# A hybrid attention backbone on one core: the opening of layer 0 rewritten, from the first load to the values

## The chip, the cores and the metric

The kernel runs on one NeuronCore of a Trainium2 chip. The metric is device time in microseconds, from one execution of the program. The engines are TensorE (PE in the profile, with its weight loads as PEld), VectorE (DVE), ScalarE (ACT), GpSimd (POOL) and SyncE (SP), which issues most of the DMAs. Each engine takes its own instructions in order and waits for others by semaphores.

## The reference

The model has two layers over 1024 latent tokens and 256 context tokens of width 1024. The opening that this case is about computes, for layer 0, the adaptive norm of both streams and then the projection to queries, keys, values and gates. Values are the first columns to be projected.

```python
shift_x, scale_x, gate_x = adaln(c, ada_w[i], ada_b[i])
shift_c, scale_c, gate_c = adaln(c_ctx, ada_w[i], ada_b[i])
hx = rms_norm(x, norm_g[i]) * (1.0 + scale_x[:, None]) + shift_x[:, None]
hc = rms_norm(ctx, norm_g[i]) * (1.0 + scale_c) + shift_c
...
q, k, v, g = jnp.split(h @ w_in, [A_WIDTH, A_WIDTH + A_KV_WIDTH, A_WIDTH + 2 * A_KV_WIDTH], axis=-1)
```

Here `adaln` is `silu(cond) @ w + bias` split into three parts of 1024 columns. Layer 0 goes on with windowed attention with a sink, layer 1 with latent attention, and a last RMS norm ends the model. All inputs are float32. Products that need full precision are split into a high and a low part (`hi` is the value rounded to the type float32r, `lo` the rest), and three products of the parts (`mm3`: L126, L127, L128) take the place of one.

## The kernel before

Tokens are in ten tiles of 128 (two of context, then eight latent), and tiles are handled in five pairs `p`. For each tile, `norm_x` (L174 to L182) loads 128 x 1024 values, squares and sums them on ACT (L178), makes the factor `(mean + eps) ** -0.5` in two small POOL operations (L179, L180), and multiplies the tile by it on DVE (L181). `turn_x` transposes the tile on TensorE in eight pieces of 128 x 128 (L188) and copies them from PSUM with ACT (L189), so that channels lie on partitions. `build_h` then applies scale and shift for each 128 channels, on DVE in place (L202), rounds two channel blocks to `hi` on ACT (L205), and subtracts to get `lo` on DVE or POOL (L207).

Scale and shift come from `ada_mm`: the weight matrix is 1024 x 2048 here, loaded in halves `h` of 512 columns for scale and for shift. The stationary operand is the two conditioning columns, so a product fills two rows of PSUM (rows 0 and 32, L337). `ada_cols` copies the rows from PSUM on ACT (L341), transposes them (L344) and adds the bias and the norm's weight. The first half's columns are ready before the second half's weights have all been loaded. `half0` builds four channel blocks of h for pairs 0 and 1, and multiplies them into the values' sums, which stay open in PSUM until the second half is done. Pairs 2 to 4 run through `build_x`, `build_h` and `proj_a`.

The weights of the projection are cut into ten blocks of 256 columns. Block 0 holds the values (1280 to 1536) and is multiplied with tokens on the output's partitions; its sums are split into hi and lo in `V` (L121, L122). Block 1 (query columns) and those behind it are turned the other way (`proj_t`): the first piece of a block covers the context in products of 256 columns, the next two pieces cover the latent tokens in products of 512. `fetch` loads a block's weights in four pieces and `cut` splits them on ACT and POOL, driven by `next_item`, which counts the pieces of work. `ada_vec` computes what is left of both layers' conditioning on DVE (L383, L385), one or two steps a piece.

Up to the end of block 0 a scheduler orders each engine's instructions. From the loop over `order` on, `tc.manual_schedule()` keeps the order in which the code is written.

Of the kernel before, what the change touches and what calls it, by code (L numbers as in the profile page):

```python
# [18 lines left out]
D = 1024  # L19
# [4 lines left out]
NP = TOK // 256  # L24
EPS = 1e-6
# [34 lines left out]
def kernel(ctx: ExitStack, tc: tile.TileContext, t, out, dbg=None):  # L60
# [58 lines left out]
    def split(hi, lo, src, lo_eng=None):  # L119

        nc.scalar.copy(hi, src)  # L121
        (lo_eng or nc.vector).tensor_sub(lo, src, hi.bitcast(F32))  # L122

    def mm3(o, a, b, first, last):
        (ah, al), (bh, bl) = a, b
        nc.tensor.matmul(o, ah, bh, start=first, stop=False)  # L126
        nc.tensor.matmul(o, al, bh, start=False, stop=False)  # L127
        nc.tensor.matmul(o, ah, bl, start=False, stop=last)  # L128
# [69 lines left out]
    def build_h(p, xt, hT, A, B, fast=False, ks=range(8)):  # L198

        w = 1 if p == 0 else 0  # L200
        for k in ks:
            nc.vector.tensor_scalar(xt[:, k, :], xt[:, k, :], A[:, k, w : w + 1], B[:, k, w : w + 1], ALU.mult, ALU.add)  # L202
            if k % 2:
                hi = hT[:, 0, k - 1 : k + 1, :]
                nc.scalar.copy(hi, xt[:, k - 1 : k + 1, :])  # L205
                eng = nc.vector if fast or k % 4 == 1 else nc.gpsimd
                eng.tensor_sub(hT[:, 1, k - 1 : k + 1, :], xt[:, k - 1 : k + 1, :], hi.bitcast(F32))  # L207
# [43 lines left out]
    cosa = f_at(0, SEQ)  # L251
    sina = f_at(10, SEQ)
    stg = Ring(F, [4, 6, 8], 512)
    xr = Ring(F, [14, 18, 48], 1024)
    xtr = Ring(F, [22, 30], 2048)
    ev = Ring(F, [38, 40, 42, 44, 46], 512)
    junk = f_at(12, 512).bitcast(BF16)
    stg_0, xr_0 = Ring(F, [4, 6], 512), Ring(F, [14, 18], 1024)
    qst = Ring(F, [34, 48], 1024)

    def src0(i):
# [44 lines left out]
        later(1, second)  # L306
        later(2, lambda: cut(3))

    def fetch0(h):
        wt[0] = r_at(wst[0], 2, 8, 256)  # L310
        load_w(wt[0], w_in, stg_0, 4 * h + 4, 256, col0=blocks[0], k0=4 * h)

    ada0 = AdaLN(0)
    ada1 = AdaLN(1)


    aring = Ring(F, [38, 8, 42, 48, 0, 30, 34, 38, 42, 8, 48, 0, 38, 42, 8, 48], 1024)
    am = f_at(46, 512)
    aw = {}

    def ada_load(h, j):
        for what in (1, 0):
            w = aw[h, j, what] = shp(aring.next(), 2, 512)
            c0 = what * D + h * 512
            src = t["ada_w"][0, j * 256 : j * 256 + 256, c0 : c0 + 512].rearrange("(k p) n -> p k n", p=128)
            if h == j == 0:
                for i in range(2):
                    load(out=w[:, i, :], in_=src[:, i, :])
            else:
                load(out=w, in_=src)  # L330

    def ada_mm(h, j):
        for i in range(2):
            k = 2 * j + i
            for what in (1, 0):
                o = PB[0:2, h, :] if what else PB[32:34, h, :]
                nc.tensor.matmul(o, sc[:, k, :], aw[h, j, what][:, i, :], start=k == 0, stop=k == 7)  # L337

    def ada_cols(h):
        for r in (0, 32):  # L340
            nc.scalar.copy(am[r : r + 2], PB[r : r + 2, h, :])  # L341
        mt = pst()[:, 0:136]
        for j in range(4):
            nc.tensor.transpose(mt[:, 34 * j : 34 * j + 34], am[0:34, j * 128 : j * 128 + 128], ident[0:34, 0:34])  # L344
        mt = shp(mt, 4, 34)
        ada0.set_cols(mt[:, :, 0:2], 1, h)
        ada0.set_cols(mt[:, :, 32:34], 0, h)


    def ada_vec():  # L350
# [65 lines left out]
        a.set_cols(shp(mt, 4, 33)[:, :, 0:33:32], cb // 2, cb % 2)  # L416

    ada_steps = ada_vec()

    def proj_mm(bi, p, j, o, ka, kb):  # L420

        h, W, js = hT[p], wt[bi], slice(j * 128, j * 128 + 128)
        for k in range(ka, kb):
            mm3(o, [h[:, s, k, js] for s in range(2)], [W[:, s, k, :] for s in range(2)], k == 0, k == 7)

    def proj_a(bi, p):
        ps = pss()
        os = [ps[:, j * 256 : j * 256 + 256] for j in range(2)]
        for j in range(2):
            proj_mm(bi, p, j, os[j], 0, 8)  # L430
        proj_out(bi, p, os)

    def proj_out(bi, p, os):
        for j in range(2):
            ti = 2 * p + j
            split(V[:, ti, :, 0:64], V[:, ti, :, 64:128], shp(os[j], 4, 64))


    hw = [None]
# [272 lines left out]
    banks0 = [[PB[:, 2 + 2 * p + j, 0:256] for j in range(2)] for p in range(2)]  # L712
    early = [shp(xtr.next(), 8, 256) for _ in range(2)]
    nx = []

    def half0(p, h):
        ks = range(4 * h, 4 * h + 4)
        build_h(p, early[p], hT[p], ada0.A, ada0.B, fast=True, ks=ks)
        for j in range(2):
            proj_mm(0, p, j, banks0[p][j], ks[0], ks[-1] + 1)  # L720

    nc.vector.memset(am[0:34], 0.0)
    ada_load(0, 0)
    load_small()
    ada_load(0, 1)
    nx.append(norm_x(src0(0), xr_0, junk))
    ada_load(0, 2)
    nx.append(norm_x(src0(1), xr_0, junk))
    ada_mm(0, 0)
    ada_load(0, 3)  # L730
    ada_mm(0, 1)
    turn_x(nx[0], early[0], 0)
    fetch0(0)
    ada_mm(0, 2)
    turn_x(nx[1], early[0], 1)
    nx.append(norm_x(src0(2), xr_0, junk))
    ada_load(1, 0)
    ada_mm(0, 3)
    ada_load(1, 1)
    ada_cols(0)  # L740
    nx.append(norm_x(src0(3), xr_0, junk))
    ada_mm(1, 0)
    ada_load(1, 2)
    half0(0, 0)
    turn_x(nx[2], early[1], 0)
    fetch0(1)
    ada_mm(1, 1)
    ada_load(1, 3)
    turn_x(nx[3], early[1], 1)
    nx.append(norm_x(src0(4), xr_0, junk))  # L750
    half0(1, 0)
    ada_mm(1, 2)
    ada_mm(1, 3)
    ada_cols(1)
    half0(0, 1)
    proj_out(0, 0, banks0[0])
    half0(1, 1)
    proj_out(0, 1, banks0[1])
    xts = {2: shp(xtr.next(), 8, 256)}
    turn_x(nx[4], xts[2], 0)  # L760
    turn_x(norm_x(src0(5), xr_0, junk), xts[2], 1)
    for p in range(2, NP):
        next_item()
        if p + 1 < NP:
            xts[p + 1] = build_x(p + 1, src0, xr, xtr, junk)
        build_h(p, xts.pop(p), hT[p], ada0.A, ada0.B)
        if p == 3:
            fetch(1)
        proj_a(0, p)
    load(out=cosa, in_=t["cos_a"])  # L770
    load(out=sina, in_=t["sin_a"])
    started = {0, 1}

    in_order = tc.manual_schedule()
    in_order.__enter__()
    for bi, gp, c in order:
        next_item()
        if bi + 1 < 10 and bi + 1 not in started:
            started.add(bi + 1)
            fetch(bi + 1)  # L780
        steps(ada_steps, 1 if gp and blocks[bi] < 1536 else 2)
        if (bi, gp, c) == (9, 2, 0):
            load2(out=mask, in_=t["mask"])
            load2(out=gx, in_=gate_d[0, 0, :].partition_broadcast(128))
            load2(out=gc, in_=gate_d[0, 1, :].partition_broadcast(128))
        if (bi, gp) == (8, 0):
            units[0].prep_q()
            units[0].prep()
            units[1].prep_q()
        if (bi, gp) == (9, 0):  # L790
            units[1].prep()
            units[2].prep_q()
            for h in range(4):
                units[0].score(h)
        r = proj_t(bi, gp, c)
        if rest:
            rest()
        rest = r
        if bi >= 8 and gp != 1:
            for _ in range(2):  # L800
                next(wo_fill, None)
# [762 lines left out]
```

## Time and profile before

| | us |
|---|---|
| median of 3 runs | 1635.42 |
| range of the 3 runs | 1634.37 to 1638.62 |
| the profiled execution | 1636.26 |
| its span | 1634.4 |
| mean granted TensorE clock | 0.992 |

The span is what the trace covers; the profiled execution's time has 1.9 us around it. Rows of the profile give a start, a duration, the engine, the line of the kernel, the operation, what it writes and reads, and in brackets how long the engine was idle before and what released it. `arena_f` is the float32 work memory, `arena_r` the float32r one (h, weights, keys and values), `PB` the PSUM, `small` a tile of small columns. A product of two full float32 operands leaves two TensorE records.

### The profile page before, as it was taken

How to read it: one execution, taken by the hardware profiler on the slowest of the kernel's cores; microseconds unless marked ns; L12 is line 12 of the kernel's file. 1: busy time of each engine (PE TensorE's matmuls, PEld its weight loads, DVE VectorE, ACT ScalarE, POOL GpSimd, SP SyncE). 2: the span in 40 equal slices, each digit the busy share in tenths (PEclk: the TensorE clock that was granted, in tenths of full speed). 3: DMA queues.
4: the chain of work that ended last, by engine and by line, in shares of the span. 5: the costliest groups of instructions: out<-in, count | busy, mean ns of one | idle time of the engine just before them, and what ended most of it. 6: DMA issues, size and time to landing. Idle time of an engine off the chain costs nothing.

```text
span 1634.4 us, 23549 instructions
## 1 busy us (share of the span) xinstructions
PE 1582.0 (97%) x8156; PEld 1212.4 (74%) x8156; DVE 955.5 (58%) x1729; ACT 813.5 (50%) x1735; POOL 806.7 (49%) x863
## 2 busy tenths in 40 slices
PE   7899999989999999999999999999999999999998
PEld 2687888777888888878887887666756766666687
DVE  1786868637767777768353015655545455455354
ACT  3622121239777777777233334555555555555421
POOL 1453446225553444435254423686676768668510
PEclk9999999999999999999999999999999999999999
DMA  7535545464333333344137613111110110122151
GB/s 275 164 119 191 196 136 174 161 189 123 104 118 97 91 95 92 99 128 134 52 101 272 194 62 108 57 56 33 39 53 22 51 38 33 54 73 70 47 161 65
DMA packets 122462, 176.72 MB, mean 108 GB/s; under 512 B 11484, under 2 KB 71516, under 8 KB 122344
## 3 DMA queue, kind: packets, MB, share of 16 engines
q1 hardware_dynamic: 115064, 164.31, 31.6%
q10 hardware_dynamic: 7280, 10.92, 2.1%
q8 instruction: 64, 1.05, 0.3%
q14 instruction: 54, 0.44, 0.1%
HBM read 129.04 MB, written 46.15 MB: 107 GB/s over the span
## 4 chain that ended last, share of the span: by engine, by line
PE 81%; DVE 5%; ACT 5%; issue 4%; POOL 3%; DMA 2%; ACTq 0%; POOLq 0%; DVEq 0%; SPq 0%
PE PB L126 17%; PE PB L128 17%; PE PB L127 17%; PE PB L1237 9%; PE PB L629 5%; PE PB L1203 4%; PE PB L619 4%; PE PB L592 2%; PE PB L593 2%; ACT arena_f L1222 1%; PE PB L1262 1%; DVE arena_f L202 1%; DVE arena_f L385 1%; ACT arena_f L640 1%; PE PB L188 1%
## 5 line engine op out<-in xcount | busy, mean ns | idle before, releaser
L126 PE MATMUL PB<-arena_r 128*128 128x512 f32 (+3 forms) x1632 | 606.5, 372 | 4.7 <-ACT arena_r L205 3.1
L127 PE MATMUL PB<-arena_r 128*128 128x512 f32 (+3 forms) x1632 | 596.3, 366 | 4.6 <-DVE arena_r L207 3.3
L128 PE MATMUL PB<-arena_r 128*128 128x512 f32 (+3 forms) x1632 | 593.8, 366 | 0.2 <-DVE arena_r L122 0.2
L126 PEld LDWEIGHTS PB<-arena_r 128*128 128x128 f32 (+1 forms) x1632 | 309.8, 190 | 95.0 <-issue 32.0
L1229 POOL TENSOR_TENSOR arena_f<-arena_f 128x512 f32<-128x512 f32 x252 | 327.2, 1298 | 75.1 <-ACT arena_f L1222 59.9
L128 PEld LDWEIGHTS PB<-arena_r 128*128 128x128 f32 (+1 forms) x1632 | 309.0, 190 | 50.7 <-issue 1.7
L127 PEld LDWEIGHTS PB<-arena_r 128*128 128x128 f32 (+1 forms) x1632 | 310.3, 190 | 47.1 <-DVE arena_r L207 4.8
L1207 DVE TENSOR_REDUCE arena_f<-PB 128x1 f32<-128x1280 f32 x128 | 190.5, 1488 | 104.1 <-PE PB L1203 101.6
L1222 ACT ACTIVATE arena_f<-PB 128x512 f32<-128x512 f32 x320 | 188.8, 597 | 125.1 <-PE PB L128 112.3
L122 DVE TENSOR_TENSOR arena_r<-PB,arena_r 128x512 fp32r<-128x512 f32 (+4 forms) x255 | 162.9, 646 | 128.1 <-ACT arena_r L121 126.3
L122 POOL TENSOR_TENSOR arena_r<-arena_f,arena_r 128x512 fp32r<-128x512 f32 x82 | 114.3, 1408 | 175.8 <-ACT arena_r L121 156.5
L121 ACT CAST arena_r<-PB 128x512 fp32r<-128x512 f32 (+4 forms) x255 | 139.1, 549 | 77.2 <-PE PB L619 39.1
L599 DVE CUSTOM_DVE_ANT_0 arena_f<-PB,arena_f,small 128x256 f32<-128x256 f32 (+1 forms) x288 | 145.5, 524 | 31.5 <-PE PB L593 24.6
L1237 PE MATMUL PB<-arena_f 128*64 128x512 f32 x640 | 157.1, 600 | 0.0
L600 ACT ACTIVATE arena_f<-arena_f,small 128x640 f32<-128x640 f32 (+2 forms) x160 | 118.9, 743 | 27.6 <-DVE small L599 26.7
L629 PE MATMUL PB<-arena_r 128*128 128x512 f32 x336 | 120.7, 435 | 4.5 <-ACT arena_f L640 4.1
L385 DVE SCALAR_TENSOR_TENSOR arena_f<-arena_f,small 128x512 f32<-128x512 f32 x98 | 114.9, 1218 | 3.9 <-DMA arena_f<-ada_w 3.6
L619 PE MATMUL PB<-ident,arena_f 128*128 128x128 f32 x672 | 104.9, 273 | 0.5 <-ACT arena_f L600 0.3
L121 ACT CAST arena_r<-arena_f 128x512 fp32r<-128x512 f32 (+1 forms) x120 | 70.0, 608 | 69.4 <-DMA arena_f<-a_w_in 21.0
L1237 PEld LDWEIGHTS PB<-arena_f 128*64 128x64 f32 x640 | 43.5, 136 | 80.9 <-issue 79.4
L1203 PE MATMUL PB<-arena_r 96*128 96x512 f32 (+1 forms) x384 | 99.8, 368 | 0.3 <-DVE arena_f L1207 0.2
L619 PEld LDWEIGHTS PB<-ident,arena_f 128*128 128x128 f32 x672 | 82.6, 140 | 15.0 <-ACT arena_f L600 1.5
(150 smaller groups left out, 1724.3 us busy)
## 6 DMA issues: line engine op xcount, KB each, us to landing
arena_r<-q_d SPq DMA_DIRECT2D x148, 128.0 KB, 2.9
arena_f<-ada_w SPq DMA_DIRECT2D x68, 256.0 KB, 3.3
arena_f<-a_w_in SPq DMA_DIRECT2D x40, 256.0 KB, 3.1
arena_f<-x SPq DMA_DIRECT2D x16, 512.0 KB, 4.8
q_d<-arena_f SPq DMA_DIRECT2D x16, 512.0 KB, 3.2
qn_d<-arena_f SPq DMA_DIRECT2D x16, 512.0 KB, 5.7
arena_r<-qn_d SPq DMA_DIRECT2D x32, 256.0 KB, 3.6
arena_f<-ada_w SPq DMA_DIRECT2D x14, 512.0 KB, 9.6
```

The costliest lines, as they stand in the source:

```text
L121: nc.scalar.copy(hi, src)
L122: (lo_eng or nc.vector).tensor_sub(lo, src, hi.bitcast(F32))
L126: nc.tensor.matmul(o, ah, bh, start=first, stop=False)
L127: nc.tensor.matmul(o, al, bh, start=False, stop=False)
L128: nc.tensor.matmul(o, ah, bl, start=False, stop=last)
L619: nc.tensor.transpose(pt[:, h, :], self.Ps[h][:, ci * 128 : ci * 128 + 128], ident)
L629: nc.tensor.matmul(self.pv, V[:, self.chunks[ci], self.g, :], PT[:, s], start=ci == 0 and s == 0, stop=ci == self.m - 1 and s == 1,)
L1203: nc.tensor.matmul(psm[:, n0 : n0 + n], self.qT[0:96, 0, b * 128 : b * 128 + 128], kt[0:96, 0, n0 : n0 + n], start=True, stop=True,)
L1207: nc.vector.reduce_max(self.mx[:, 96 + b : 97 + b], psm[:, 0:TOK], AX.X, negate=True)
L1222: nc.scalar.activation(E, S, AF.Exp)
L1229: eng.tensor_add(self.acc, self.acc, E)
L1237: nc.tensor.matmul(self.pv[p : p + 64], Vq[:, c, self.h % 4, :], self.E.pop(c), start=c < 2, stop=c >= NT - 2)
```

## The change

Everything between the loading of constants and the loop over `order` is replaced, and now lies under the manual schedule as well.

- **Scale and shift.** All 2048 columns are taken in one pass over the eight 128-row pieces, each loaded as two DMAs of 128 x 1024 into a ring of three buffers. The four groups of 512 columns go to four parts of 32 columns of TensorE's array and so to rows 0, 32, 64 and 96 of one PSUM bank. One copy, four transposes of 128 x 128 and three DVE operations make all columns of scale (A) and shift (B).
- **Norm and turn.** The tile is no longer multiplied by its factor. Instead a diagonal matrix is made from the identity (L704, 128 x 128), and one float32 product of a tile's piece with the diagonal both normalises and transposes it (L716).
- **h from PSUM.** A part `g` is a pair `p` and two channel blocks; its four turned pieces fill one of six PSUM banks. `h_part` reads the bank: ACT writes `hi` (L728), DVE writes the unrounded h to a small ring (L729), two of each per part, and DVE or POOL subtracts (L730).
- **Values.** `v_part` multiplies a part into the pair's values two parts later, both tiles' sums sharing bank 4 or 5 by turns. Turns run two parts ahead.
- The values' weights come in two DMAs and are cut in four steps; block 1's weights are fetched at part 7 and cut at parts 10 and 13; cosine and sine are loaded at parts 11 and 12.

```diff
+    def ada_load(k):
+        aw[k] = awr.next()
+        for c in (0, 1024):
+            load(out=aw[k][:, c : c + 1024], in_=t["ada_w"][0, k * 128 : k * 128 + 128, c : c + 1024])
+
+    def ada_mm(k):
+        for q in (0, 1, 2, 3):
+            nc.tensor.matmul(
+                PA[32 * q : 32 * q + 2], sc[:, k, :], aw[k][:, q * 512 : q * 512 + 512], start=k == 0, stop=k == 7
+            )
...
+    def norm(i):
+        st = sm_ring()
+        nc.scalar.activation(junk, xn[i][0], AF.Square, accum_out=st[:, 0:1])
+        nc.gpsimd.tensor_scalar(st[:, 1:2], st[:, 0:1], 1.0 / D, EPS, ALU.mult, ALU.add)
+        nc.gpsimd.tensor_tensor(st[:, 2:3], st[:, 1:2], mhalf, ALU.pow)
+        xn[i][1] = dg.next()
+        nc.vector.tensor_scalar_mul(xn[i][1], ident, st[:, 2:3])
...
+    def turn(g):
...
+                nc.tensor.matmul(
+                    bank(g)[:, kk, j * 128 : j * 128 + 128], x[:, c0 : c0 + 128], d, start=True, stop=True
+                )
+
+    def h_part(g, eng):
...
+        for kk in range(2):
+            k = 2 * b + kk
+            sa, sb = ada0.A[:, k, w : w + 1], ada0.B[:, k, w : w + 1]
+            nc.scalar.activation(hi[:, kk], bank(g)[:, kk], AF.Identity, bias=sb, scale=sa)
+            nc.vector.tensor_scalar(h[:, kk], bank(g)[:, kk], sa, sb, ALU.mult, ALU.add)
+        eng.tensor_sub(hT[p][:, 1, 2 * b : 2 * b + 2, :], h, hi.bitcast(F32))
...
+    in_order = tc.manual_schedule()
+    in_order.__enter__()
...
+    NG = 4 * NP
+    for g in range(NG + 2):
+        p, b = g // 4, g % 4
+        if 4 <= g + 2 < NG:
+            turn(g + 2)
+        if g < NG:
+            h_part(g, nc.gpsimd if g % 2 else nc.vector)
+        if b < 2 and p + 1 < NP:
+            norm(2 * p + 2 + b)
+        if b == 2 and 0 < p and p + 2 < NP:
+            x_load(2 * p + 4)
+            x_load(2 * p + 5)
+        if g >= 2:
+            v_part(g - 2)
+        if g == 7:
+            next_item()
+            fetch(1)
+        if g in (10, 13, 16):
+            next_item()
```

On VectorE, where the first h is made, stood before (L202 scales and shifts in place, L181 multiplies a tile by its factor, L207 subtracts; the brackets name the semaphores of the engines waited for):

```order
L171 SCALAR_TENSOR_TENSOR small<-small 128x8 [waits DVE_49]
L202 TENSOR_SCALAR arena_f<-arena_f,small 128x256 [waits DVE_49]
L202 TENSOR_SCALAR arena_f<-arena_f,small 128x256 x2
L181 TENSOR_SCALAR arena_f<-arena_f,small 128x1024 [waits DMAHW3_49,Activation_49,Pool_49]
L207 TENSOR_TENSOR arena_r<-arena_f,arena_r 128x512 [waits Activation_49]
L202 TENSOR_SCALAR arena_f<-arena_f,small 128x256
L207 TENSOR_TENSOR arena_r<-arena_f,arena_r 128x512 [waits Activation_49]
```

and at the same place, over the first pair's parts, stands now (L704 makes a diagonal):

```order
L729 TENSOR_SCALAR arena_f<-PB,small 128x256 [waits DMAHW3_49,Activation_49]
L729 TENSOR_SCALAR arena_f<-PB,small 128x256 [waits Activation_49]
L730 TENSOR_TENSOR arena_r<-arena_f,arena_r 128x512 [waits DVE_49]
L704 TENSOR_SCALAR arena_f<-ident,small 128x128 [waits Pool_49]
L729 TENSOR_SCALAR arena_f<-PB,small 128x256 [waits Activation_49] x2
L704 TENSOR_SCALAR arena_f<-ident,small 128x128 [waits Pool_49]
L729 TENSOR_SCALAR arena_f<-PB,small 128x256 [waits DMAHW4_49,Activation_49]
L729 TENSOR_SCALAR arena_f<-PB,small 128x256 [waits Activation_49]
L730 TENSOR_TENSOR arena_r<-arena_f,arena_r 128x512 [waits DVE_49]
```

A scaling in place, which at this spot waits for no other engine, became a read of PSUM that waits for ACT each time, and diagonals that wait for POOL stand between the readings.

On ScalarE, over the first parts, stands now (L677 copies the ada rows, L700 squares a tile):

```order
L677 COPY arena_f<-PB 128x512 [waits DMAHW4_49,DVE_49,PE_49]
L728 ACTIVATE arena_r<-PB,small 128x256 [waits DVE_49] x2
L700 ACTIVATE arena_f,small<-arena_f 128x1024 [waits DMAHW1_49,Activation_49]
L728 ACTIVATE arena_r<-PB,small 128x256
L728 ACTIVATE arena_r<-PB,small 128x256 [waits DVE_49]
L700 ACTIVATE arena_f,small<-arena_f 128x1024 [waits DMAHW2_49,Activation_49]
L728 ACTIVATE arena_r<-PB,small 128x256
L728 ACTIVATE arena_r<-PB,small 128x256 [waits DVE_49]
```

The second of a part's two ACT readings waits for DVE's first; before, ACT's roundings (L205) waited for DVE's scalings and no DVE scaling waited for them.

On TensorE, behind the last ada product, stands now (L679 transposes the ada rows):

```order
L672 MATMUL PB<-arena_f,small 2x512 [waits DMAHW0_49]
L672 MATMUL PB<-arena_f,small 2x512
L679 MATMUL PB<-ident,arena_f 128x128 [waits Activation_49]
L679 MATMUL PB<-ident,arena_f 128x128 x3
L716 MATMUL PB<-arena_f 128x128 [waits DMAHW1_49,DVE_49]
L716 MATMUL PB<-arena_f 128x128 [waits DMAHW2_49,DVE_49]
L716 MATMUL PB<-arena_f 128x128 x2
L126 MATMUL PB<-arena_r 128x256 [waits Activation_49]
L127 MATMUL PB<-arena_r 128x256
L128 MATMUL PB<-arena_r 128x256 [waits Pool_49]
```

The fifth part's turn, which needs the diagonals of tiles 2 and 3, stands ahead of the first product of values; before, values of the first half stood ahead of the second half's ada products.

More of the change, by code (lines that the diff above doesn't have):

```diff
@@ L307, in fetch @@
         later(2, lambda: cut(3))
-    def fetch0(h):
-        wt[0] = r_at(wst[0], 2, 8, 256)
-        load_w(wt[0], w_in, stg_0, 4 * h + 4, 256, col0=blocks[0], k0=4 * h)
     ada0 = AdaLN(0)
     ada1 = AdaLN(1)
[L317 to L347, printed above, removed]
     def ada_vec():
@@ new lines, in x_load, with bank @@
+    def x_load(i):
+        xn[i] = [xs.next(), None]
+        load(out=xn[i][0], in_=src0(i))
+    def norm(i):
[5 more added lines that the diff above has]
+        nc.vector.tensor_scalar_mul(xn[i][1], ident, st[:, 2:3])
+    def bank(g):
+        return shp(PB[:, turned[g % 6], :], 2, 256)
@@ new lines @@
+    ada_load(1)
+    x_load(0)
+    x_load(1)
+    ada_load(2)
+    w0_load(0)
+    ada_mm(0)
+    ada_mm(1)
+    norm(0)
+    norm(1)
+    ada_mm(2)
+    ada_load(3)
+    w0_load(1)
+    w0_cut(0)
+    w0_cut(1)
+    for g in range(2):
+        turn(g)
+    ada_load(4)
+    ada_mm(3)
+    ada_load(5)
+    for g in range(2, 4):
+        turn(g)
+    w0_cut(2)
+    w0_cut(3)
+    for k in (6, 7):
+        ada_load(k)
+        ada_mm(k - 2)
+    for i in range(2, 6):
+        x_load(i)
+    ada_mm(6)
```

136 lines of the change are left out of this document (60 added, 76 removed).

## The prediction

> **What bounds the kernel now.** The page comes first: its busy times tell which engine the whole waits for. Then the stretches of ten microseconds, for the part that the change rewrites (columns: busy time and instructions of PE, PEld, DVE, ACT, POOL, then granted clock, DMA share, GB/s).
>
> ```profile
> PE 1582.0 (97%) x8156; PEld 1212.4 (74%) x8156; DVE 955.5 (58%) x1729; ACT 813.5 (50%) x1735; POOL 806.7 (49%) x863
> ...
> 0.00:10.00 10.00, 5.00 (x8) 0.46 (x8) 0.63 (x5) 1.71 (x3) 0.20 (x4) 1.00 0.75 218
> 10.00:20.00 10.00, 7.64 (x27) 1.64 (x26) 0.93 (x2) 3.27 (x6) 1.26 (x4) 1.00 1.05 392
> 20.00:30.00 10.00, 6.02 (x26) 2.93 (x27) 3.86 (x10) 5.45 (x10) 3.54 (x5) 0.85 0.93 341
> 30.00:40.00 10.00, 9.77 (x44) 3.94 (x42) 0.92 (x2) 2.31 (x5) 0.74 (x2) 0.81 0.47 163
> 50.00:60.00 10.00, 6.70 (x34) 5.59 (x33) 7.91 (x15) 7.17 (x14) 5.13 (x5) 0.72 0.65 216
> 90.00:100.00 10.00, 10.00 (x72) 9.35 (x71) 5.52 (x9) 3.26 (x7) 2.23 (x2) 1.00 0.00 0
> ```
>
> TensorE is busy 97% of the span and from 90 us on full, so what the opening gains or loses moves the rest as a whole. Inside the opening the DMA is full from 10 to 30 us and half idle after that, and the clock falls to 0.72 in one stretch: a chain of loads, norms and products, no full engine. The mark by which I compare is the first product of 512 columns, block 1's second piece; all 288 products of 256 columns (240 of values, 48 of block 1's first piece) stand before it in both kernels.
>
> ```profile
> 96.33 0.40 PE L126 MATMUL PB<-arena_r 128*128 128x512 f32 x1
> ...
> L126 PE MATMUL PB<-arena_r 128*128 128x256 f32 x96 | 28.4, 308 | 3.1 <-ACT arena_r L205 3.1
> ```
>
> The mark is at 96.3 us now (96 products on each of three lines).
>
> **Loads.** All of ada_w's scale and shift, ctx and the values' weights (8 + 1 + 1 MiB, with the small tables 10.6 MB) must land before the last ada product; no h can be made earlier. The rows give 2.2 MB by 10 us and 392 GB/s when the queue is full; the remaining 8.4 MB take 21.5 us: **31.5 us**. Three 1 MiB buffers hold the stream: the fourth load waits for the first product, but 3.5 MiB stand in the queue by then, so I see no gap. The old order had scale and shift of the first half at 26 us and of the second at 52 us (the first L202 of each, below).
>
> **Columns.** The chain behind the last ada product, as it runs now:
>
> ```profile
> 26.69 1.06 DVE L202 TENSOR_SCALAR arena_f<-arena_f,small 128x256 f32<-128x256 f32 x3
> ...
> 29.14 0.41 DVE L202 TENSOR_SCALAR arena_f<-arena_f,small 128x256 f32<-128x256 f32 x1
> ...
> 48.44 1.88 PE L337 MATMUL PB<-arena_f,small 128*2 128x512 f32 x8
> 50.37 1.16 ACT L341 COPY arena_f<-PB 2x512 f32<-2x512 f32 x2 [4.91 <-PE PB L337]
> 51.59 0.43 PE L344 MATMUL PB<-ident,arena_f 34*128 34x34 f32 x4 [1.00 <-ACT arena_f L341]
> 52.46 2.99 DVE L202 TENSOR_SCALAR arena_f<-arena_f,small 128x256 f32<-128x256 f32 x6
> ```
>
> From 50.3 to 52.5 us with two copies; one copy (0.58) goes and the transposes grow from 34 to 128 columns: 1.8 us. Ahead of it stand the products on the last landed half, 1 to 1.9 us by clock (eight records took 1.88 in two column parts). Scale and shift are ready at **35.3 us**.
>
> **The parts.** Now twenty parts, each with two ACT and two DVE passes over one PSUM bank. In the built order, shown above, the four alternate: each DVE pass waits for the ACT pass, the second ACT pass for the first DVE pass. The old value split already does this when its two halves share a bank:
>
> ```profile
> 64.20 1.07 DVE L122 TENSOR_TENSOR arena_r<-PB,arena_r 128x256 fp32r<-128x256 f32 x3
> ...
> 91.04 0.41 DVE L122 TENSOR_TENSOR arena_r<-PB,arena_r 128x256 fp32r<-128x256 f32 x1
> 91.49 0.37 ACT L121 CAST arena_r<-PB 128x256 fp32r<-128x256 f32 x1 [2.74 <-DVE arena_r L122]
> 91.89 0.42 DVE L122 TENSOR_TENSOR arena_r<-PB,arena_r 128x256 fp32r<-128x256 f32 x1 [0.44 <-ACT arena_r L121]
> ...
> 30.23 0.69 DVE L207 TENSOR_TENSOR arena_r<-arena_f,arena_r 128x512 fp32r<-128x512 f32 x1 [0.69 <-ACT arena_r L205]
> 61.64 0.19 POOL L179 TENSOR_SCALAR small<-small 128x1 f32<-128x1 f32 x1 [1.95 <-ACT arena_f L178]
> 61.92 0.55 POOL L180 TENSOR_TENSOR small<-small 128x1 f32<-128x1 f32 x1
> ...
> 97.07 1.67 ACT L121 CAST arena_r<-arena_f 128x512 fp32r<-128x512 f32 x3
> 97.77 4.70 POOL L122 TENSOR_TENSOR arena_r<-arena_f,arena_r 128x512 fp32r<-128x512 f32 x3 [8.26 <-ACT arena_r L121]
> ...
> L178 ACT ACTIVATE arena_f<-arena_f 128x1024 bf16<-128x1024 f32 x10 | 10.6, 1059 | 11.7 <-DMA arena_f<-ctx 10.7 <-DMA arena_f<-x 1.0
> L207 POOL TENSOR_TENSOR arena_r<-arena_f,arena_r 128x512 fp32r<-128x512 f32 x6 | 8.5, 1425 | 11.3 <-ACT arena_r L205 11.3
> ```
>
> ACT starts 0.04 us after DVE's end, DVE 0.03 after ACT's. So from DVE's first pass of a part to that of the next: 0.41 + 0.04 + 0.37 + 0.03 and the second pass's 0.34 to the next start (three in a row took 1.07), 1.2 us; on even parts DVE's subtraction adds 0.6. Two parts take 3.0 us, a pair of tiles (four parts) 6.0.
>
> Two norms lie in each of the first four pairs. The first puts square 1.06, read 0.19 and POOL's 0.8 ahead of the diagonal that DVE must make (0.25 at most, from 0.41 for twice the columns) before its next pass: 2.4 us where 1.1 went, +1.3. For the second POOL does an odd part's subtraction (1.4) first: 2.9 for 0.4, +2.5. A split of values costs four alternating passes, two of which stand in DVE's way between: +1.2. The three cuts of block 1's weights put three pieces of 512 columns, 1.7 us on ACT and 4.7 on POOL by the rows at 97 us, ahead of later norms: about +1 in the third pair and +1.7 in the fourth. Pairs: 9.8, 11.0, 12.0, 12.7 and, without norms, 7.2: 52.7 us.
>
> Three moved steps I cost at nothing. The x tiles are loaded two at a time when their buffer's turn is done, and normed two parts later:
>
> ```profile
> arena_f<-x SPq DMA_DIRECT2D x16, 512.0 KB, 4.8
> ```
>
> Two parts are 5.5 us at the pace above, so 4.8 is hidden by 0.7; a full queue would cost about a microsecond a pair. Block 1's weights are fetched behind them at the eighth part and cut by the fourteenth, some 20 us before their first product. Cosine and sine come behind these on SP and are first read at L489, after the mark. If any of the three came late, block 1 would wait for it alone.
>
> **TensorE beside it.** Paces from neighbouring starts and from long rows:
>
> ```profile
> 85.18 0.28 PE L128 MATMUL PB<-arena_r 128*128 128x256 f32 x1
> 85.30 0.28 PE L126 MATMUL PB<-arena_r 128*128 128x256 f32 x1
> ...
> 63.93 1.04 PE L188 MATMUL PB<-ident,arena_f 128*128 128x128 f32 x8
> ...
> 1083.33 4.51 PE L1237 MATMUL PB<-arena_f 128*64 128x512 f32 x20
> ```
>
> A value product takes 0.12, a transpose 0.11. The turning product is a full fp32 product. L1237's are the nearest row: two records each, 0.41 us a record in its half of the array, for 512 columns; for 128 columns that is 0.11, so a product is two records, 0.22. Below that it can't go by these rows; were the weight load not hidden, 0.05 more a record. A part thus costs 0.9 for the turn and 1.4 for the values, 2.3; a pair 9.2, under DVE's 11 to 12.7. But values come late after a half-clock start. The fifth turn needs the diagonals of tiles 2 and 3, about 41 to 43 us; TensorE has stood some six microseconds by then. The rows at 20 and 50 us show the clock falling in thin stretches. I take 5 us at half. The first pair's split then waits for TensorE and holds DVE some 2.4 us, and the last pair's split some 2.
>
> **Sum.** 35.3 for scale and shift, 0.4 for ACT's first pass, 52.7 for the pairs, 4.4 for the two waits: DVE's last pass ends at 92.8. POOL's last subtraction 1.4, twelve products 1.4, block 1's first piece 48 x 0.12 = 5.8: the mark is at **101.4 us** instead of 96.3, **+5.1**. The copies and norms that go (twenty copies, forty scalings, ten multiplications of 1024) stood on ACT and DVE, which now do ten times 3.0 us of alternating passes instead. TensorE's work grows: 64 products in place of 64 transposes after 42 us, 7 us more.
>
> Behind the mark the program is the same. The gates' first pieces now come later on DVE, since their loads wait for the last part's buffer:
>
> ```profile
> 107.44 0.69 DVE L489 TENSOR_TENSOR arena_f<-PB,arena_f 128x512 f32<-128x512 f32 x1 [1.76 <-PE PB L128]
> 124.36 1.68 PE L396 MATMUL PB<-arena_f,small 128*1 128x512 f32 x4 [0.33 <-DVE arena_f L385]
> ```
>
> DVE had 1.8 us to spare at 107 us, so one microsecond of lateness is hidden; past that TensorE would wait at the row of 124 us. I take nothing, at most 2. The profiled execution took 1636.26 us; with 5.1 it is 1641.4, and since the median lies 0.84 lower, **1640.5 us**.
>
> **What the skill says against the change.** The Trainium skill (PSUM — Partial Sum Buffer, PSUM bank collisions raise a hardware error) says that ScalarE and VectorE may not touch one bank in the same partitions at once, reads included, so software must serialise them. The split rows agree: each pass starts 0.03 to 0.04 us after the other's end. If the passes could overlap, the parts would hide under TensorE's 2.3 us, and the sum would be the first rival's below.
>
> **Rivals.** *TensorE bounds it.* If ACT's and DVE's passes from PSUM are shorter than the split's, or the norms slip between them, only TensorE's work is left: 16 x 0.9 + 240 x 0.12 from 42 us, 2.5 lost to the clock, 5.8: the mark at 93.5, **1632.6 us**, 1629 if loads come a microsecond earlier and the clock is full. For it: the pace of a pair is only a fifth above TensorE's. Against it: the waits in the built order.
>
> *The clock stays up.* Now turning is done by products. Then the ada products end 0.9 us earlier and the two waits nearly go: the mark at 97.5 to 98.5, **1637 us**. For it: the row at 10 us shows full clock with as thin a load; against it the stand before the fifth turn. The Trainium skill (TensorE: Matmul & The Clock Gate, Part 4: PE-mode transpose) says that transposes do not count as busy for the clock; by that rule the new products would, but its Part 1 has one idle window of 3.4 us bring the half clock back. No row here tells transposes apart.
>
> *The four column parts do not run side by side.* The trace shows only two. If they go two by two, an ada step is two pairs of two records, 1.7 us at 0.43 a record, 3.4 at half clock, against 2.7 for its 1 MiB at 392 GB/s, and the loads stall behind their buffers: 31.5 becomes 34 to 37, **1645 us**. It decides as soon as a step exceeds 2.7 us.
>
> **How the numbers follow.** Forecast 0.50 (1637.5 to 1644), TensorE bound 0.22, clock up 0.18, parts in turn 0.10. A measurement of this kernel tells 0.3%, 4.9 us, from no change. Slower by more: 0.42 of the forecast and the last, 0.52. Faster by more: the lower half of the first rival, 0.10. Between: 0.38. The range leaves out that lower half and the far end of the last: 1632 to 1646.
>
> **What would show it.** In the new profile: the last ada load near 31.5 us; L728 idle behind L729 and L729 behind L728; the fifth turn near 42 us and a clock row under 1.00 there; pairs of tiles 11 to 12.7 us apart; a mark near 101 us. Wrong it would be if TensorE has no gaps from 45 us on (first rival), or if ada products follow each other without waiting for DMA (third).

## The result and the profile after

The changed kernel takes 1646.24 us (median of 4 runs, 1645.10 to 1647.91) against 1635.45 us for the kernel before: the ratio is 1.0064, with a 95% interval of 1.0046 to 1.0081. Slower, as forecast, but by 10.8 us where 5.1 were forecast. The median lies 0.2 us above the top of the forecast's range, 1646, which is less than the runs of one kernel differ. The profiled execution took 1645.10 us, 8.8 more than before's. It is the fastest of the four, and the account below explains what it shows; the other 2 us of the 10.8 stand in no profile.

The first fence is the page's busy line and the stretches of ten microseconds of the changed kernel, with the columns of before's (busy time and instructions of PE, PEld, DVE, ACT, POOL, then clock, DMA share, GB/s).

```profile
PE 1583.2 (96%) x8232; PEld 1222.1 (74%) x8232; DVE 948.1 (58%) x1724; ACT 810.8 (49%) x1732; POOL 807.9 (49%) x865
...
20.00:30.00 10.00, 8.99 (x53) 2.84 (x51) 1.37 (x2) 1.14 (x2) 1.27 (x1) 1.00 1.03 407
30.00:40.00 10.00, 3.83 (x16) 1.10 (x14) 3.05 (x9) 3.90 (x8) 0.78 (x2) 0.81 0.58 231
40.00:50.00 10.00, 6.92 (x47) 6.92 (x47) 5.12 (x10) 5.47 (x11) 4.00 (x6) 0.68 0.00 0
60.00:70.00 10.00, 6.68 (x48) 6.49 (x47) 4.58 (x11) 5.43 (x12) 4.08 (x6) 0.84 0.29 106
70.00:80.00 10.00, 9.95 (x71) 9.76 (x69) 6.43 (x10) 6.83 (x14) 7.21 (x7) 0.81 0.55 185
90.00:100.00 10.00, 7.69 (x60) 7.09 (x59) 4.53 (x9) 3.40 (x8) 3.48 (x4) 1.00 0.06 11
```

From 30 to 100 us TensorE is nearly full in two stretches only (9.95 of 10 us from 70 to 80, at a clock of 0.81, and 9.49 from 50 to 60), no other engine is full in any, and the DMA is more than half idle: a chain of waits sets the pace, and now it lasts longer. TensorE, full from 90 us on before, still stands for 2.3 us between 90 and 100. The timeline gives the mark, and behind it the later row that both kernels share (L355 now, L396 before):

```profile
105.52 0.40 PE L126 MATMUL PB<-arena_r 128*128 128x512 f32 x1
133.55 1.68 PE L355 MATMUL PB<-arena_f,small 128*1 128x512 f32 x4 [0.33 <-DVE arena_f L344]
```

The mark moved from 96.3 to 105.5 us, +9.2, and the row behind it by the same 9.2. All of this loss arises ahead of the mark, and nothing is given back or added in the 28 us behind it. (The span grew by 8.7, so 0.5 is given back later.) Next is the chain of waits of the changed kernel, in order of time, over parts 2 and 3 (start, us, what; L702 makes a tile's factor, "issue" is time without a visible wait):

```profile
42.15 0.56 POOL small L702
...
42.95 0.55 DVE arena_f L729
43.52 0.57 ACT arena_r L728
44.12 0.56 DVE arena_f L729
44.70 0.04 DVE arena_r L730
44.73 0.57 issue
45.31 0.55 DVE arena_f L729
45.88 0.58 ACT arena_r L728
46.48 1.01 DVE arena_f L729 x2
```

ACT and DVE take turns at a bank with 0.02 to 0.05 us between them. DVE's first pass of part 2 starts at 42.95, that of part 3 at 45.31 and that of part 4 inside the last row at 46.94: two parts without a norm cost 4.0 us, where the forecast had 3.0. The part whose subtraction is on DVE takes 2.36 of them, the other 1.63: two passes of DVE with one of ACT between. From 34.77 us (first L728) to 96.95 (end of the last L729) the chain runs through such passes, norms on POOL, diagonals and splits; TensorE is in it nowhere. (From 92.9 to 97.0 us the view gives only "issue"; DVE's own rows show the same turns there.) The groups of the changed kernel between 30 and 100 us, shapes apart (busy, mean ns of one, then idle time by releaser):

```profile
L728 ACT ACTIVATE arena_r<-PB,small 128x256 fp32r<-128x256 f32 x40 | 21.6, 563 | 21.9 <-DVE arena_f L729 20.7 <-DVE small L691 1.3
L729 DVE TENSOR_SCALAR arena_f<-PB,small 128x256 f32<-128x256 f32 x40 | 21.3, 542 | 14.0 <-ACT arena_r L728 13.9
L716 PE MATMUL PB<-arena_f 128*128 128x128 f32 x128 | 20.6, 305 | 13.7 <-DVE arena_f L704 13.7
```

A pass takes 0.56 us on ACT and 0.54 on DVE, where the forecast took 0.37 and 0.41, and each engine idles behind the other. TensorE stands 13.7 us for diagonals. In the timeline these are the first turns of the pairs (for pair 1 one wait for each of its tiles):

```profile
38.87 0.79 PE L716 MATMUL PB<-arena_f 128*128 128x128 f32 x2 [4.65 <-DVE arena_f L704]
43.09 1.65 PE L716 MATMUL PB<-arena_f 128*128 128x128 f32 x6 [3.42 <-DVE arena_f L704]
54.67 0.94 PE L716 MATMUL PB<-arena_f 128*128 128x128 f32 x6 [0.51 <-DVE arena_f L704]
67.57 1.65 PE L716 MATMUL PB<-arena_f 128*128 128x128 f32 x6 [3.32 <-DVE arena_f L704]
81.75 0.94 PE L716 MATMUL PB<-arena_f 128*128 128x128 f32 x6 [1.80 <-DVE arena_f L704]
...
98.35 0.39 PE L127 MATMUL PB<-arena_r 128*128 128x256 f32 x1 [1.28 <-POOL arena_r L730]
```

After the stands of 3.3 and 3.4 us six records take 1.65 us, after the shorter ones 0.94: the half clock comes back within the opening (granted clock 0.84 from 60 to 70 us, 0.81 from 70 to 80), which the forecast had only once.

### The profile page after: what moved, and what is told of

It reads as the page before. It is cut to its first block, busy times and chain, and to the rows that moved or that the text cites. A ratio compares the mean times of both kernels' runs of the same rounds, so it can differ in the third digit from the quotient of the medians.

```text
span 1643.1 us, 23681 instructions
## 1 busy us (share of the span) xinstructions
PE 1583.2 (96%) x8232; PEld 1222.1 (74%) x8232; DVE 948.1 (58%) x1724; ACT 810.8 (49%) x1732; POOL 807.9 (49%) x865
## 4 chain that ended last, share of the span: by engine, by line
PE 81%; DVE 6%; ACT 4%; DMA 3%; issue 3%; POOL 2%; SPq 0%; ACTq 0%; POOLq 0%; DVEq 0%
PE PB L126 17%; PE PB L128 17%; PE PB L127 16%; PE PB L1279 9%; PE PB L570 5%; PE PB L1245 4%; PE PB L560 4%; PE PB L533 2%; PE PB L534 2%; DMA arena_f<-ada_w 2%; DVE arena_f L729 1%; DVE arena_f L344 1%; PE PB L1304 1%; DVE arena_r L122 1%; ACT arena_f L1264 1%
## 5 line engine op out<-in xcount | busy, mean ns | idle before, releaser
L1249 DVE TENSOR_REDUCE arena_f<-PB 128x1 f32<-128x1280 f32 x128 | 190.4, 1488 | 103.9 <-PE PB L1245 101.4
```

The costliest lines, as they stand in the source:

```text
L1249: nc.vector.reduce_max(self.mx[:, 96 + b : 97 + b], psm[:, 0:TOK], AX.X, negate=True)
```

## The experiments

Two questions were open: whether the alternation on one bank is what the parts cost (and why it costs more than forecast), and how the chain beside it, through TensorE and POOL, comes in. The mark is read from each kernel's own trace. The loads do not end at the same time in every execution: the shift was ready between 34.2 and 35.5 us. So the table also gives the time from there (the end of L691) to the mark; the forecast had 66.1. The kernel before, run again beside the experiments, took 1637.0 to 1637.2 us, and the ratios of e1 to e11 are to these runs.

| run | mark, us | shift ready to mark, us | time, us | ratio to before, 95% |
|---|---|---|---|---|
| before | 96.3 | | 1635.45 | 1 |
| changed kernel | 105.5 | 70.8 | 1646.24 | 1.0064 (1.0046 to 1.0081) |
| e1 readings together | 100.4 | 65.6 | 1643.18 | 1.0040 (1.0025 to 1.0054) |
| e2 copy and addition | 104.7 | 69.2 | 1646.52, one run | |
| e3 values and splits ahead | 115.0 | 80.6 | 1654.92 | 1.0112 (1.0097 to 1.0127) |
| e4 subtractions on DVE | 107.0 | 72.1 | 1647.49 | 1.0064 (1.0049 to 1.0079) |
| e5 products ahead | 105.0 | 70.7 | 1645.05 | 1.0050 (1.0034 to 1.0067) |
| e6 = e2 + e5 | 96.8 | 62.5 | 1635.90, one run | |
| e7 = e1 + e5 | 97.1 | 62.9 | 1636.39 | 0.9998 (0.9988 to 1.0007) |
| e8 = e7, diagonals later | 102.4 | 68.1 | 1641.77 | 1.0031 (1.0018 to 1.0045) |
| e9 = e7, POOL for the norms | 88.6 | 54.3 | 1629.51 | 0.9955 (0.9941 to 0.9968) |
| e10 constants for columns | 104.0 | 69.2 | 1643.62, one run | |
| e11 = e9, alternating again | 104.0 | 68.5 | 1642.96 | 1.0039 (1.0025 to 1.0053) |

**e1: the readings of an engine together.**

```diff
...
             nc.scalar.activation(hi[:, kk], bank(g)[:, kk], AF.Identity, bias=sb, scale=sa)
+        for kk in range(2):
+            k = 2 * b + kk
+            sa, sb = ada0.A[:, k, w : w + 1], ada0.B[:, k, w : w + 1]
             nc.vector.tensor_scalar(h[:, kk], bank(g)[:, kk], sa, sb, ALU.mult, ALU.add)
```

> Edit: in a part, ACT's two readings of the bank stand together and DVE's two behind them, so that ACT reads the next part's bank while DVE reads this one. Theory A (the alternation on one bank is the bound; in the changed kernel the chain of waits goes L728, L729, L728, L729 from 34.8 to 97.0 us, 4.0 us for two parts without a norm): two parts then cost DVE 1.0 + 0.7 + 1.0 = 2.6 to 2.7 us, a pair with norms about 10.5 instead of 13, the last pair about 8; the first product of 512 columns comes at 93 to 97 us instead of 105.5, and the time is 9 to 12 us shorter, about 1635. Rival B (the norms' chain square, POOL, diagonal sets the pace and would with any order): 105.5 less 2 at most, 1644 to 1646. Rival C (TensorE bounds it already): no change, 105.5.

The mark came 5.1 us earlier, so the alternation costs, but only half of what theory A gave: the mark was expected at 93 to 97. The chain of waits of e1 shows what took over (L728 and L732 are the readings, L733 the subtraction):

```profile
41.90 0.30 DVE arena_f L704
42.24 1.65 PE PB L716 x6
...
53.04 0.14 PE PB L128
53.20 0.38 ACT arena_r L121
53.60 0.44 DVE arena_r L122
54.06 0.37 ACT arena_r L121
54.43 0.94 ACT arena_r L728 x2
55.39 1.01 DVE arena_f L732 x2
```

A pair's second diagonal releases a turn, behind it stand three more turns and the 48 products of the pair before, the split waits for the last of these, and ACT's and DVE's next readings stand behind the split.

**e2: the forecast's passes.** ACT copies, DVE adds the identity; scale and shift are left out.

```diff
-            nc.scalar.activation(hi[:, kk], bank(g)[:, kk], AF.Identity, bias=sb, scale=sa)
-            nc.vector.tensor_scalar(h[:, kk], bank(g)[:, kk], sa, sb, ALU.mult, ALU.add)
+            nc.scalar.copy(hi[:, kk], bank(g)[:, kk])
+            nc.vector.tensor_tensor(shp(h[:, kk], 2, 128), shp(bank(g)[:, kk], 2, 128), ident.unsqueeze(1).to_broadcast([128, 2, 128]), ALU.add)
```

> Edit: the same passes in the same order without the scale and shift columns: ACT copies from the bank, DVE adds a constant tile to it; this leaves scale and shift out of h. The forecast took 0.37 us for ACT's pass and 0.41 for DVE's from the split of values; 0.56 and 0.54 were measured. Theory A (the column operands make the passes longer, and the passes' length is the term that was too small): the passes fall to 0.36 to 0.42, two parts without a norm take 3.0 us instead of 4.0, the mark comes at 95 to 98 us instead of 105.5, unless TensorE becomes the bound at about 94. Rival B (reading 128 x 256 from PSUM out of this place costs 0.55 whatever the operation): passes stay above 0.5, mark 105 to 106. Rival C (passes are shorter but something else ends the parts): passes 0.4, mark above 101.

Rival C. The passes fell to 374 and 421 ns, yet the mark came only 0.8 us earlier, and 1.6 counted from the ready shift. With the forecast's own passes the forecast's own mark, 101.4, was not reached. TensorE's row tells why:

```profile
79.20 1.65 PE L716 MATMUL PB<-arena_f 128*128 128x128 f32 x6 [3.21 <-DVE arena_f L704]
```

Ready values stand behind this turn, the six records take 1.65 us instead of 0.94, and in the last pair the readings stop for the split from 87.0 us to 92.4.

**e10: the same operations with constants.** Scale and shift are left out here too.

```diff
-            nc.scalar.activation(hi[:, kk], bank(g)[:, kk], AF.Identity, bias=sb, scale=sa)
-            nc.vector.tensor_scalar(h[:, kk], bank(g)[:, kk], sa, sb, ALU.mult, ALU.add)
+            nc.scalar.activation(hi[:, kk], bank(g)[:, kk], AF.Identity, scale=2.0)
+            nc.vector.tensor_scalar(h[:, kk], bank(g)[:, kk], 2.0, 1.0, ALU.mult, ALU.add)
```

> Edit: the changed kernel's passes, the same two operations in the same order, with constants in place of the scale and shift columns (this leaves scale and shift out of h). e2 changed the operation too (a copy and an addition). Theory A (reading the columns makes a pass 0.13 to 0.19 us longer): the passes fall to 0.36 to 0.43 as in e2. Rival B (the operation itself is slower out of PSUM than a copy or an addition): they stay at 0.54 to 0.57. The mark then is as in e2, 104 to 105.5, by A, and unchanged at 105 to 106 by B.

```profile
L729 DVE TENSOR_SCALAR arena_f<-PB 128x256 f32<-128x256 f32 x40 | 16.5, 420 | 10.1 <-ACT arena_r L728 10.1
L728 ACT ACTIVATE arena_r<-PB 128x256 fp32r<-128x256 f32 x40 | 14.5, 383 | 21.2 <-DVE arena_f L729 20.0 <-PE PB L716 1.3
```

Theory A, with the mark at the edge of its range: without columns the same operations take 383 and 420 ns, with them 563 and 542. The two columns cost 180 ns on ACT and 122 on DVE. That is the size that the forecast missed; the split's passes, from which it took its price, read no columns. The Trainium skill (ScalarE: Activation LUTs, What ACT_TABLE_LOAD costs) gives some 93 ns for each column that an activation reads; the 180 ns for two agree with it, and the forecast had not used it.

**e3: values ahead, with their splits.**

```diff
+        if g >= 2:
+            v_part(g - 2)
         if 4 <= g + 2 < NG:
             turn(g + 2)
...
-        if g >= 2:
-            v_part(g - 2)
```

> Edit: in the loop over the parts the values of part g - 2 stand ahead of the turn of part g + 2 on TensorE. The forecast put 4.4 us on TensorE: a fifth turn that holds the values back until 44 us, a half clock, and two splits of values that wait for it. Theory A (TensorE is nowhere on the path between 34.8 and 98.3 us, as the chain of waits of the changed kernel has it): the first product of values moves from 44.4 to about 38 to 39 us and TensorE's stand gets shorter, but the mark stays at 105.5 within 0.7 and the time within 2 us. Rival B (the late values hold the splits and through them DVE, as forecast): the mark comes 2 to 4.4 us earlier, 1641 to 1644. Rival C (a turn now comes late for its part, since the values stand ahead of it): the mark comes 1 to 3 us later.

None of the three. The edit moved more than was meant: `v_part` holds the split of the values as well, and this moved ahead of the part's readings on ACT and DVE. Now they wait for TensorE in each pair, as here in ACT's timeline:

```profile
51.45 0.37 ACT L121 CAST arena_r<-PB 128x256 fp32r<-128x256 f32 x1 [2.58 <-PE PB L128]
```

The mark came 9.5 us later. The run alone says nothing about the order on TensorE. Against e5 below, which moves the products and leaves the split where it was, it says what the split's place costs: 10 us over five pairs, some 2 us a pair.

**e4: all subtractions on DVE.**

```diff
-            h_part(g, nc.gpsimd if g % 2 else nc.vector)
+            h_part(g, nc.vector)
```

> Edit: DVE makes all twenty subtractions; POOL has only the norms' small operations and the weight cuts. Theory A (the chain through ACT and DVE is the bound, and POOL's subtraction of 1.3 us ahead of the second norm of a pair adds its own part to it): each second norm's diagonal comes 0.9 to 1.2 us earlier (four pairs, -4), the odd subtractions of the other parts cost DVE up to 0.6 each (six, +3.6), the last subtraction ends 0.6 earlier: the mark at 103.5 to 105.5, the time 0 to 2 us shorter. Rival B (POOL is the bound of the parts): 5 us shorter or more, mark at 100 or earlier. Rival C (DVE alone is the bound): twenty times 0.6 less ten already there, 6 us longer, mark at 110 or later.

The mark came 1.5 us later: between A and C. DVE's wait ahead of each second diagonal fell from 2.3 us to 0.7, and DVE, which is in the chain, got ten subtractions more.

**e5: only the products ahead.** The split is taken out of `v_part` and stays in its place.

```diff
+        if g >= 2:
+            v_part(g - 2)
         if 4 <= g + 2 < NG:
             turn(g + 2)
...
-            v_part(g - 2)
+            v_split(g - 2)
```

> Edit: only the products of values of part g - 2 stand ahead of the turn of part g + 2 on TensorE; the split of a pair's values stays where it was on ACT and DVE (in e3 it moved ahead of the part's own readings). Theory A (two chains of nearly one length: the alternation of ACT and DVE, 62.2 us from 34.8 to 97.0 without a step of TensorE in it, and beside it a loop diagonal, turn, values, split, whose wait ends just before): taking TensorE's waits away alone brings little, the mark comes at 104 to 105.6 instead of 105.5, the time within 1.5 us of the changed kernel's. Rival B (TensorE's standing behind late diagonals is what bounds): the mark at 102 or earlier. Rival C (the turns come late): mark past 106.5.

Theory A: 105.0, 0.5 us earlier, but these 0.5 lie ahead of the first reading; counted from the ready shift the gain is 0.1. TensorE's waits alone are not what bounds the changed kernel.

**e6: e2 and e5 together** (without scale and shift).

> Edit: e2 and e5 together: passes without scale and shift (this leaves them out of h), and the products of values ahead of the turn. e2's passes took 0.37 and 0.42 us, just as the forecast had them, and its mark still came at 104.7. Theory A (in e2 the second chain took over: each pair's first turn waits for a diagonal, ready values stand behind it, the split waits for them, and a half clock follows the stand): with both gone the forecast's chain is left, 0.4 + 52.7 us from 34 to 35 us, then 1.4 and 7.2: mark at 94 to 97. Rival B (the norms' chain through POOL bounds e2): mark at 101 or later.

Theory A, at the edge of its range: 96.8. Counted from the ready shift that is 6.8 us earlier than e2, while e5 alone brought 0.1. With its passes and without TensorE's waits the forecast's chain is there: 62.5 us from the ready shift to the mark, where the forecast without its 4.4 for those waits comes to 61.7. The five pairs (from first L728 to first L728, the last to the end of L729) take 10.7, 11.1, 11.9, 13.1 and 8.4 us, where the forecast had 9.8, 11.0, 12.0, 12.7 and 7.2. (In the first pair ACT's first pass no longer waits for the columns and DVE's still does; that is 0.9 of the 10.7.)

**e7: e1 and e5 together.**

> Edit: e1 and e5 together: the two readings of each engine stand together, and the products of values ahead of the turn. e1's mark came at 100.4; its chain ran diagonal, turn, values, split, readings, POOL, diagonal. Theory A (that loop is cut when ready values no longer stand behind the turn): TensorE's own work is nearly all that is left: first values at 38 to 39 us, 16 turns of 0.95 and 240 products of 0.12 are 44 us, 2.5 lost at half clock, 5.8 for block 1's first piece: mark at 91 to 95, time 1631 to 1635, at or below the kernel before. Rival B (the norms' chain on POOL still holds the parts): mark at 98 or later, 1639 or more.

97.1 lies between the theories: 8.4 us ahead of the changed kernel, most of the 9.2 that the change lost, and the time can't be told from before's. Behind a turn and products at half pace from 41.6 to 47 us, what holds it back now is POOL, which its chain of waits shows best between 60 and 76 us:

```profile
60.18 1.28 POOL arena_r L733
61.46 0.08 issue
61.55 0.19 POOL small L701
...
66.18 1.73 POOL arena_r L122
67.91 1.22 issue
69.13 1.72 POOL arena_r L733
...
71.20 0.56 POOL small L702
...
71.99 1.00 DVE arena_f L732 x2
```

POOL: a subtraction ahead of the norm, then three cuts of block 1's weights and a subtraction behind them ahead of the next norm.

**e8: the diagonals one part later.** e7 with this, and the turn behind the diagonal in the code:

```diff
-        xn[i][1] = dg.next()
+        xn[i][1] = st
+
+    def diag(i):
+        st, xn[i][1] = xn[i][1], dg.next()
         nc.vector.tensor_scalar_mul(xn[i][1], ident, st[:, 2:3])
...
+        if 0 < b < 3 and p + 1 < NP:
+            diag(2 * p + 1 + b)
         if b < 2 and p + 1 < NP:
             norm(2 * p + 2 + b)
+        if 4 <= g + 2 < NG:
+            turn(g + 2)
```

> Edit: e7, and each diagonal is made by DVE one part later, behind that part's readings, the turn behind it in the code. Theory A (DVE's waits for POOL's factor, 12 us in ten waits in the changed kernel, are taken off the path): mark 1 to 3 us earlier than e7's, at 90 to 93, time 1629 to 1632. Rival B (with e7 TensorE is the bound and these waits are hidden): mark within 0.7 of e7's. Rival C (turns come too late when they wait for a diagonal made a part later): mark later than e7's by 1 or more.

Rival C: 5.3 us later than e7. In the chain of waits the diagonal at 54.26 us releases the turn, with all values behind it, up to the split at 61.65. DVE no longer waits for POOL, but TensorE waits 8.1 us for diagonals, where it waited 2.1 in e7.

**e9: POOL for the norms.** e7 with this:

```diff
-            h_part(g, nc.gpsimd if g % 2 else nc.vector)
+            h_part(g, nc.gpsimd if g in (3, 7, 15) else nc.vector)
```

> Edit: e7, and POOL keeps only the subtractions of parts 3, 7 and 15; DVE makes the other seventeen, so that POOL is free for the second norm of each pair and for the three weight cuts at part 10. e7's mark came at 97.1, its chain went through POOL's subtraction, factor, diagonal, split four times, and through 4.2 us of cuts and a subtraction behind them. Theory A (the norms' chain on POOL bounds e7): each second diagonal comes about a microsecond earlier and the part behind the cuts about 2, mark at 91 to 94.5, time 1630 to 1634, faster than the kernel before. Rival B (e7 is bound by TensorE with its half clock at 38 to 46 us and its seven short stands): mark within 1 us of 97. Rival C (DVE, with 0.7 us more in seven parts, becomes the bound, as in e4, whose mark came 1.5 us later than the changed kernel's): mark at 98 or later.

Theory A, and more than it: the mark at 88.6, 8.4 us ahead of e7 and 7.7 ahead of the kernel before. The theory's terms reached only to 91; where the other 2.4 us come from was not separated. The stretches of e9:

```profile
40.00:50.00 10.00, 10.00 (x85) 10.00 (x85) 7.78 (x17) 6.45 (x15) 3.09 (x5) 0.97 0.08 18
50.00:60.00 10.00, 10.00 (x89) 10.00 (x88) 8.12 (x18) 7.38 (x17) 3.64 (x6) 1.00 0.62 218
60.00:70.00 10.00, 10.00 (x89) 10.00 (x88) 8.47 (x14) 7.35 (x17) 6.67 (x8) 1.00 0.67 241
70.00:80.00 10.00, 9.62 (x80) 9.22 (x79) 8.81 (x17) 5.40 (x13) 2.77 (x4) 1.00 0.09 26
```

TensorE is full from 40 us on but for 0.24 us at 71.9, at nearly full clock. It is the one version that beats both kernels: 1629.51 us, 0.9955 of before.

**e11: e9 with the alternation back.** The readings stand as in the changed kernel.

> Edit: e9 with the readings back in the changed kernel's order (ACT, DVE, ACT, DVE on one bank); products ahead of the turn and POOL kept for the norms as in e9, whose mark came at 88.6 with TensorE busy without a stand from 41 us on. Theory A (the alternation on one bank alone is enough to keep TensorE waiting): a part costs 2.36 us by its readings, 9.4 a pair, diagonals 0.6, a split of about 1.2 and waits for norms of 1 to 2 on top, 11.5 to 13 a pair against TensorE's 9.2: the mark at 99 to 105, 1639 to 1646. Rival B (POOL's work and the order on TensorE were the loss, the alternation only came beside it): mark within 3 us of e9's, below 92.

Theory A: 104.0, 15.3 us behind e9; 1.15 of these lie ahead of the first reading, which came at 35.55 us instead of 34.40, so 14.2 are the alternation's. (The 2.36 us that the expectation gives to a part's readings hold DVE's subtraction too.) So the alternation by itself is enough to hold the opening within 2.3 us of the changed kernel's length, whatever is mended elsewhere. Taking it away alone (e1) gives 5.1 us, since the order on TensorE (e7) and POOL (e9) bound next.

## Why the prediction was half right

**Loads, columns: right.** The products of the last landed half ran at 31.86 us (forecast 31.5), and the columns were ready at 34.7 (35.3, though its terms add up to 35.2 at most):

```profile
31.86 1.03 PE L672 MATMUL PB<-arena_f,small 128*2 128x512 f32 x4 [0.25 <-DMA arena_f<-ada_w]
...
34.56 0.17 DVE L691 TENSOR_TENSOR small<-PB,small 128x16 f32<-128x16 f32 x1
```

**The alternation: the mechanism right, the pass too short.** This term of the sum was mis-sized. The forecast took its passes from the split's rows, 0.37 and 0.41, and gave two parts 3.0 us; with scale and shift columns they are 0.56 and 0.54, and two parts take 4.0. Ten times 1.0 is 10 us too little. That the columns make the difference is shown by e10; that the alternation makes a pass count at all, by e9 against e11.

**The two waits for TensorE: not in this chain, and elsewhere too small.** In the changed kernel no wait for TensorE is in the chain; e5, which puts ready products ahead of the waiting turn, gained 0.1 us. So the sum was 4.4 us too long here. But the waits are hidden rather than absent: with the forecast's passes (e2, e10) it is 69.2 us from the ready shift to the mark, 3.1 more than the forecast's 66.1. The forecast let TensorE stand once, ahead of the fifth turn; in the changed kernel it stands ahead of the first turn of every pair but the first, because each of these waits for a diagonal.

So two steps were off, and either alone brings the mark late (e5 has only the longer passes, e2 and e10 only TensorE's stands). Shorter passes alone take 1.6 from the changed kernel's 70.8 us, products ahead on TensorE alone 0.1, both together by 8.3 (e6). That the forecast's error in time was no larger is partly luck: 10 us too little for the passes stood against 4.4 for waits that the longer passes cover.

**Norms and splits: right within a microsecond, as a sum.** From the first L728 to the end of the last L729 the forecast had 57.5 us; with 10 more for the passes and without the 4.4 it would be 63.1, and 62.2 were measured. So the chain is 4.7 us longer than forecast, and with a start 0.5 earlier the mark comes 4.1 later. The price of the weight cuts is luck in part. In the third pair no norm stood behind the cuts; the microsecond put there came from a subtraction on DVE that took 1.80 us beside them instead of 0.69 (last section). In the fourth the cuts cost some 0.7 us, where 1.7 was put.

**The moved steps at nothing: right.** No reading, norm or turn waits for an x tile, block 1's weights or a table from 35 us to the mark. From the end of DVE's last pass the mark comes 8.57 us later (8.6 forecast), and behind the mark nothing was lost (forecast nothing, at most 2).

**The rivals.** TensorE did not bound it; e9 shows what that looks like, its mark is 4.9 us earlier than the rival's 93.5, and its values begin at 35.0 us (the second product at 37.2), not behind a turn at 42. The clock did not stay up: 0.68 between 40 and 50 us, and low again behind later stands. The ada steps did not hold up the loads: a half's products took 1.03 us and the next waited 0.25 for its DMA.

One reading does not fit the forecast's own rows: "no full engine" ahead of 90 us, while TensorE was busy 9.77 of 10 us from 30 to 40. No term of the sum rests on it.

## What to carry to other kernels

Where two engines must read one PSUM bank, let each do all its reading of a bank in one go and work on different banks meanwhile: the alternation put a pass of ACT between DVE's two in every part, 1.63 us instead of the 1.0 of DVE's own two. A price taken from a similar row holds only for the same operands: look whether the row reads per-partition columns. When two chains are nearly equally long, undoing one shows little: counted from the ready shift, 5.2 and 0.1 us for e1 and e5 alone and 7.9 for both, and 1.6 for e2 alone but 8.3 with e5. Test pairs of edits before calling a part harmless.

## What the runs showed of the hardware

Reading columns has a price on both engines, 180 ns for two on ACT and 122 for two on DVE at 128 x 256 from PSUM (e10).

A subtraction of 128 x 512 with both inputs in SBUF takes DVE 0.69 us, but beside POOL's cuts in the changed kernel it took 1.80, and the reading of PSUM right behind it, with POOL still at work, 0.53. From DVE's and POOL's timelines:

```profile
70.48 4.22 POOL L122 TENSOR_TENSOR arena_r<-arena_f,arena_r 128x512 fp32r<-128x512 f32 x3 [3.29 <-ACT arena_r L121]
70.51 1.80 DVE L730 TENSOR_TENSOR arena_r<-arena_f,arena_r 128x512 fp32r<-128x512 f32 x1
72.23 0.53 DVE L729 TENSOR_SCALAR arena_f<-PB,small 128x256 f32<-128x256 f32 x1
```

The 1.1 us more is a little less than one of POOL's three operations, 1.4. In e4 and e11, where DVE's subtraction again starts 0.03 us behind POOL's first cut, it takes 1.79; in e2 and e10, where it starts 0.1 us ahead of it, the usual 0.69. The Trainium skill (SBUF — State Buffer, Terms) says that DVE and GpSimd lock a port pair for a whole instruction and the loser blocks; these rows agree, but no run was made to test it alone.

The half clock also came back behind shorter stands than the two of 3.3 and 3.4 us above: in e4 TensorE stood 2.9 us ahead of turns at 67.8 and 82.3 us, each time with one pair of records shortly before, and the granted clock was 0.50 from 69 to 71 us and 0.53 from 84 to 86.
